# A hybrid decoder trunk on one core: VectorE work moved behind GpSimd's powers, attention ranked ahead, staged loads and first splits reordered

## The chip, the core and the metric

The kernel runs on one core of a Trainium2 chip. The core has a matrix engine (TensorE, in the profile PE, its weight loads PEld), a vector engine (VectorE, DVE), a scalar engine (ScalarE, ACT), a slower general engine (GpSimd, POOL) and an engine that only issues DMAs here (SyncE, SP). Each engine works through its own instructions in order, and waits on semaphores of the others. The metric is the device time of one execution in microseconds; the kernel before and the changed kernel are compared by their medians.

## The reference, cut to what matters

Two layers of a decoder trunk, 512 tokens of width 1024, all in float32:

```python
for l in range(2):
    h = rms_norm(x, ln_mix[l])
    proj = h @ w_in[l]                     # split into the inputs of four mixers and the gates g
    y_a = gelu(a_u) * (tril(sgu_w) @ rms_norm(gelu(a_v), sgu_norm) + sgu_b)   # gMLP, chunks of 128
    y_b = dsa_attention(q, k, v, qi, ki, wi)   # q, k normed and rotated; an indexer keeps 128 keys a query
    y_c = sigmoid(c_o) * rms_norm(mlstm_chunkwise(...), mlstm_norm)           # chunks of 128
    y_d = d_b * causal_conv3(d_c * d_x)
    x += (sum_n sigmoid(g_n) * (y_n @ w_branch[l, n])) @ w_out[l]
    h = rms_norm(x, ln_mlp[l])
    x += relu(h @ w_up[l]) ** 2 @ w_down[l]    # hidden width 4096
```

The norms use 1/sqrt(mean of squares + 1e-6). The indexer's score of a query against the keys before it is sum_h w_h relu(qi_h . ki), and the 128 best keys are kept for queries from position 128 on.

## The kernel before, in words

**Layout.** Activations lie feature-major: eight tiles of 128 features by 512 tokens. Every product of float32 operands is three matmuls: each operand is split into a high and a low part (hh and hl for h, whi and wlo for weights), and high·high, high·low and low·high are added up in PSUM (`mm3`).

**Weights.** A weight chunk (1024 or 1280 columns by 128 partitions) goes through `next_w`: SP loads it into `raw` (two buffers), ACT casts `whi<-raw`, DVE subtracts `wlo<-raw,whi` (three buffers each). The end of `wlo` frees the raw buffer, and so lets SP's next weight load start. These three steps are under high priority (`HP`).

**Order of the work.** The program is written once in Python; a scheduler then sets each engine's order from data dependencies and priorities. The stream of big products is the main line. Everything else (rotations, the indexer, top-k, mLSTM chunks, softmax) is written as generators in a list `side`; `tick()`, called after each half of a product's matmuls, lets each generator go one step, up to its next `yield`. While it does, the wrapper `Paced` ties every side instruction to the latest matmul of the main line (`at["mm"]`) by a dependency that only the scheduler sees, so that side work isn't ordered ahead of its place. `Ahead` is another wrapper, for DVE and ACT: it puts one tenth of the urgent priority around each call; the mLSTM uses it before the change. All instructions issued through such a wrapper carry the wrapper's line, L139, in the profile.

**One layer of the mixer.** Token-major projections come first (`tok_proj`, tile `tk`: 512, 336, 512 columns), then feature-major ones (`fm_proj`, tile `fm`), and again token-major ones. `qk_prep` norms and rotates q (i = 0) and k (i = 1): squares, `ssq` sums, a power on POOL (`rpow`), the products `rr` and `rt` of the rotation, times ssq, transposes on PE (`qkT`). For q, ssq is also multiplied by −0.125. The powers of all norms run on POOL.
The gMLP: its gate input v lies in two tiles v20 and v21, each with two chunks of tokens side by side. `vs` holds the chunks' mean squares; after the power on POOL, four scalings multiply v by vs and 0.5, written inline on the main line. `sgu_mix`, a side generator, then multiplies the triangular matrices `wt` by v on PE (`mix`, 16 small matmuls for each of two feature tiles i).
The indexer's top-k works on a score tile `sco` with DVE alone: 16 rounds for each block of 128 queries, of MAX (the eight largest into `m`) and MATCH_REPLACE (which strikes them out; a value load goes ahead of it).
mLSTM: per chunk a state, numerators `nd`, the result `hc`; its norm is `dn`, with a power on POOL and a scaling by 0.5, then hc·dn, then times (1 + tanh of the output gate) into `h2`; `finish` transposes h2 and multiplies it by `mlstm_norm`.
Then the gates (`gates`, tiles `g` and `p`, DVE's `gs` and `mg`), with attention (`lg`, softmax in `L`, transposes `pT`, `av`) between them, and the product with w_out (`wo`).

**The MLP** runs in three passes of 12, 12 and 8 tiles of the hidden width. In each, pairs of up tiles (`up`) come first; then the down projection (tiles `q` and `r` of PE) in a form with seven products in place of eight for each 2×2 of blocks. Its weights are staged: `load` brings blocks of w_down into six buffers `cr`, by SP, or by POOL's queue (always where a load adds onto a tile), and DVE adds some; `use` splits and multiplies one. `chain` is the tile that goes through block 11, 11+12, then plus 22, then plus 21; `b22` is block 22, and in the last pass, of 8 tiles, `sum2` is block 22 plus block 12, loaded over POOL's queue. In the two passes of 12 tiles nkp is 3, in the last 2. Results of a pass are kept in DRAM (`sum_dram`), the last pass folds them into x.

**The start.** The first product's weights go chunk by chunk with x: `first_loads(k0)`, called ahead of the split of chunk k0, loads the tiles of x that the chunk needs and norms them; the first two weight chunks are in `raw01`.

Of the kernel before, what the change touches and what calls it, by code (L numbers as in the profile page):

```python
# [21 lines left out]
P = 128  # L22
# [144 lines left out]
def trunk(tc, x_in, wall, consts, lps, sgus, out):  # L167
# [5 lines left out]
    with ExitStack() as es:  # L173
# [189 lines left out]
        def mlp(l, hh, hl, r2, gain):  # L363
# [10 lines left out]
            with tc.tile_pool(name="ap", bufs=1) as ap:  # L374
# [6 lines left out]
                for p, nt in enumerate(PASSES):  # L381
                    nk = nt // 2
                    ah, al = [], []
                    for t in range(nk):
                        F = ap.tile([P, 4, 256], F32, name="F", tag="F")
                        G_ = ap.tile([P, 4, 256], F32, name="Fs", tag="Fs")
                        ah.append(ftile("ah", f"ah{t}"))
                        al.append(ftile("al", f"al{t}"))
                        for i in range(2):
                            w_h, w_l = next_w()  # L390
                            pt = mmtile("up")
                            fm_group(pt, w_h, w_l, hh, hl)
                            a = flat(F[:, 2 * i:2 * i + 2])
                            with HP():
                                S.activation(a, pt, AF.Relu)
                                S.activation(a, a, AF.Square)
                        with HP():
                            S.copy(ah[t][:, 0:3], F[:, 1:4])
                            V.tensor_sub(G_[:, 0:2], F[:, A21:A21 + 1].to_broadcast([P, 2, 256]), F[:, A11:A22 + 1])
                            V.tensor_sub(G_[:, 2], F[:, A11], G_[:, 1])  # L400
                            V.tensor_sub(G_[:, 3], F[:, A12], G_[:, 2])
                            S.copy(ah[t][:, 3:7], G_)
                            V.tensor_sub(al[t][:, 0:3], F[:, 1:4], ah[t][:, 0:3].bitcast(F32))
                            V.tensor_sub(al[t][:, 3:7], G_, ah[t][:, 3:7].bitcast(F32))
# [24 lines left out]
                    def load(dst, i, j, k, add=False, eng=nc.sync):  # L429
                        with HP():  # L430
                            if add:
                                nc.gpsimd.dma_start(dst, piece(i, j, k), accum_op=ALU.add)
                            else:
                                eng.dma_start(dst, piece(i, j, k))
# [94 lines left out]
                    for k in range(nkp):  # L529
                        load(chain[k], 1, 1, k)  # L530
# [19 lines left out]
                    if 3 * nkp <= 6:  # L550

                        sum2 = [ap.tile([P, 1024], F32, name="cr", tag="cr", bufs=6) for _ in range(nkp)]
                        for k in range(nkp):
                            load(sum2[k], 2, 2, k, eng=nc.gpsimd)
# [100 lines left out]
def mixer(tc, em, env):  # L655
# [41 lines left out]
    def tok_proj(n, kk, chunks, tags, before=None, order=KORD[0]):  # L697
        pts = {c: mmtile("tk", tags[i]) for i, c in enumerate(chunks)}
        kks = kk if isinstance(kk, tuple) else (kk,) * (KD // kk)
        for k0, kk in zip(np.cumsum((0,) + kks), kks):  # L700
            w_h, w_l = next_w(before(k0) if before else None)
            assert not env["at"]["fold"] or order[k0] > 3
# [64 lines left out]
    else:  # L767
# [3 lines left out]

        def first_loads(k0):
            ks = {0: (0, 1), 1: ()}.get(k0, (k0, k0 + 1))
            for k in ks:
                x0.append(rtile("x0").bitcast(F32))
                with HP():
                    nc.sync.dma_start(x0[k], x_in[k])
                acc[:] = [norm(x0, lp("ln_mix"), hh, hl, (k,), *acc, sq_hp=False, sq_tile=et)]
            return raw01[:, k0] if k0 < 2 else None

        pq = tok_proj(512, G1K[0], [1, 2, 3], MM4, first_loads)
# [96 lines left out]
    def attention(sel, yb):  # L878
        Ls, pTs = {}, {}
# [101 lines left out]
    def mlstm(yc):  # L981
        V, S = Ahead(tc, env["V"]), Ahead(tc, env["S"])

        def finish(c, h2):
            pk = mmtile("hT", "ms")
            mn = lp("mlstm_norm")
# [7 lines left out]
        ip, gc, gi = lfs  # L994

# [48 lines left out]
        for c in range(4):  # L1044
# [61 lines left out]
            V.tensor_scalar(dn, dn, 0.5, None, ALU.mult)  # L1106
            V.tensor_mul(hc, hc, dn.unsqueeze(2).to_broadcast([P, 4, 64]))
            h2 = hc.rearrange("p h d -> p (h d)")
            V.scalar_tensor_tensor(h2, to[:, c], 1.0, h2, ALU.add, ALU.mult)
            yield from wait(3)  # L1110
# [28 lines left out]
    def qk_prep(i, n, src):  # L1139
# [9 lines left out]
        if i == 0:  # L1149
            V.tensor_scalar(ssq, ssq, -0.125, None, ALU.mult)  # L1150
# [103 lines left out]
    for c in range(4):  # L1254
        s_ = slice((c % 2) * 256, (c % 2) * 256 + 256)
        V.tensor_scalar(v2[c // 2][:, s_], v2[c // 2][:, s_], vs[:, c:c + 1], 0.5, ALU.mult, ALU.mult)
# [190 lines left out]
```

## Time and profile before

| | |
|---|---|
| runs of the kernel before | 1593.58 us median of three (1592.1 to 1593.97) |
| the profiled execution's own time | 1594.98 us |
| its span, first to last instruction | 1593.2 us |
| granted TensorE clock, mean | 0.999 |
| busy, share of the span | PE 99%, PEld 82%, DVE 70%, ACT 44%, POOL 8% |
| DMA | 198.91 MB, 125 GB/s in the mean |
| largest groups on PE | up, g, q, r, tk: 512-column matmuls, 0.39 us each as modelled, pipelined |
| largest groups on DVE | wlo<-raw,whi: 221, 282.9 us; wlo<-cr,whi: 96, 117.0 us |

A row of a timeline gives start, length (both us), engine, line, operation, output<-inputs, shape, how many in a row, and in brackets the idle time before it and what ended that. Matmuls overlap: the length of one is modelled, the distance of two starts is what it costs. The tile names in the rows are the program's, so a wait can be found in the code by its tile.

### The profile page before, as it was taken

The numbers are of one execution on the slowest core, as the hardware profiler recorded it, in microseconds if no ns is written. First come the engines' busy times: TensorE is split into PE (matmuls) and PEld (weight loads), VectorE is DVE, ScalarE is ACT, GpSimd is POOL, SyncE is SP. The second block draws the span as 40 slices with busy tenths as digits, with TensorE's granted clock in tenths as the row PEclk, the third lists the DMA queues.
The fourth block names the chain that finished last, engine by engine and source line by source line (L and its number), as shares of the span: only waits on it lengthen the run. The fifth ranks groups of instructions, "written<-read, shape, count | busy, mean of one in ns | idle before, by whom it ended". The sixth has DMA issues, their size and how long they took to land.

```text
span 1593.2 us, 20154 instructions
## 1 busy us (share of the span) xinstructions
PE 1580.3 (99%) x7584; PEld 1303.7 (82%) x7584; DVE 1109.5 (70%) x1893; ACT 708.2 (44%) x1056; POOL 122.2 (8%) x153
## 2 busy tenths in 40 slices
PE   9999999999999999999999999999999999999999
PEld 7788887878888888878888888887888888888887
DVE  6799997555555665655987999975555557556568
ACT  5454224423336545635554532354233455455362
POOL 1221000000000100020013120000000001001200
PEclk9999999999999999999999999999999999999999
DMA  7433322242353473387345233232423534724962
GB/s 192 128 100 104 103 92 91 84 135 100 100 187 129 71 233 99 74 210 213 93 130 137 85 110 106 83 99 76 143 96 107 199 105 71 233 94 79 239 184 80
DMA packets 67058, 198.91 MB, mean 125 GB/s; under 512 B 7616, under 2 KB 14848, under 8 KB 66960
## 3 DMA queue, kind: packets, MB, share of 16 engines
q1 hardware_dynamic: 54160, 167.15, 32.0%
q0 software_dynamic: 11936, 29.45, 10.2%
q8 instruction: 60, 0.98, 0.2%
q10 hardware_dynamic: 864, 1.01, 0.2%
q14 instruction: 38, 0.31, 0.1%
HBM read 177.10 MB, written 16.81 MB: 122 GB/s over the span
## 4 chain that ended last, share of the span: by engine, by line
PE 71%; DVE 17%; issue 6%; DMA 4%; POOL 2%; ACT 1%; ACTq 0%; DVEq 0%; POOLq 0%
PE up L139 22%; PE g L139 15%; PE q L139 10%; PE r L139 7%; PE wo L139 5%; PE p L139 4%; DVE wlo L139 4%; DVE sco L139 3%; PE tk L139 3%; DMA raw<-in_wall_dram 2%; DVE m L139 2%; PE fm L139 1%; DVE X L139 1%; ACT whi L139 1%; DVE rr L139 1%
## 5 line engine op out<-in xcount | busy, mean ns | idle before, releaser
L139 DVE TENSOR_TENSOR wlo<-raw,whi 128x1024 fp32r<-128x1024 f32 (+3 forms) x221 | 282.9, 1280 | 150.0 <-ACT whi L139 149.7
L139 ACT CAST whi<-raw 128x1024 fp32r<-128x1024 f32 (+3 forms) x220 | 241.1, 1096 | 252.1 <-DMA raw<-in_wall_dram 64.9
L139 PE MATMUL g<-hh,whi 128*128 128x512 f32 x512 | 200.6, 392 | 0.0
L139 PE MATMUL up<-hh,whi 128*128 128x512 f32 x512 | 199.5, 390 | 0.7 <-ACT whi L139 0.7
L139 PE MATMUL up<-hh,wlo 128*128 128x512 f32 x512 | 199.3, 389 | 0.5 <-DVE wlo L139 0.5
L139 PE MATMUL g<-hh,wlo 128*128 128x512 f32 x512 | 199.5, 390 | 0.0
L139 PE MATMUL g<-hl,whi 128*128 128x512 f32 x512 | 199.4, 389 | 0.0
L139 PE MATMUL up<-hl,whi 128*128 128x512 f32 x512 | 199.2, 389 | 0.0
L139 DVE TENSOR_TENSOR wlo<-cr,whi 128x1024 fp32r<-128x1024 f32 x96 | 117.0, 1221 | 75.9 <-ACT whi L139 75.8
L139 ACT CAST whi<-cr 128x1024 fp32r<-128x1024 f32 x96 | 100.9, 1053 | 120.7 <-PE r L139 45.0
L139 ACT ACTIVATE gs<-gs 128x512 f32<-128x512 f32 x64 | 40.6, 634 | 195.6 <-DVE gs L139 195.4
L139 PEld LDWEIGHTS up<-hh,whi 128*128 128x128 f32 x512 | 96.1, 188 | 21.1 <-ACT whi L139 1.2
L139 PEld LDWEIGHTS up<-hh,wlo 128*128 128x128 f32 x512 | 96.1, 188 | 20.9 <-DVE wlo L139 1.0
L139 PEld LDWEIGHTS g<-hh,wlo 128*128 128x128 f32 x512 | 96.1, 188 | 20.2
L139 PEld LDWEIGHTS g<-hh,whi 128*128 128x128 f32 x512 | 96.1, 188 | 20.2 <-issue 0.3
L139 PEld LDWEIGHTS up<-hl,whi 128*128 128x128 f32 x512 | 96.1, 188 | 19.9
L139 PEld LDWEIGHTS g<-hl,whi 128*128 128x128 f32 x512 | 96.2, 188 | 19.3
L139 PE MATMUL tk<-whi,hh 128*128 128x512 f32 (+2 forms) x304 | 108.3, 359 | 0.3 <-DVE whi L139 0.3
L139 PE MATMUL tk<-wlo,hh 128*128 128x512 f32 (+2 forms) x304 | 106.9, 355 | 0.0
L139 PE MATMUL tk<-whi,hl 128*128 128x512 f32 (+2 forms) x304 | 105.9, 352 | 0.0
L139 PE MATMUL q<-whi,ah 128*128 128x512 f32 (+1 forms) x260 | 100.4, 390 | 0.0
L139 PE MATMUL q<-wlo,ah 128*128 128x512 f32 (+1 forms) x260 | 100.4, 386 | 0.0
(287 smaller groups left out, 3040.7 us busy)
## 6 DMA issues: line engine op xcount, KB each, us to landing
raw<-in_wall_dram SPq DMA_DIRECT2D x147, 512.0 KB, 3.5
raw<-in_wall_dram SPq DMA_DIRECT2D x64, 640.0 KB, 3.8
cr<-in_wall_dram POOLq DMA_DIRECT2D x36, 512.0 KB, 5.4
cr<-in_wall_dram SPq DMA_DIRECT2D x32, 512.0 KB, 5.1
x<-in_x_dram SPq DMA_DIRECT2D x16, 256.0 KB, 5.0
xm_dram<-x SPq DMA_DIRECT2D x16, 256.0 KB, 2.0
sum_dram<-co SPq DMA_DIRECT2D x16, 256.0 KB, 4.4
sum_dram<-co POOLq DMA_DIRECT2D x16, 256.0 KB, 6.9
```

What stands on the lines that cost most here:

```text
L139: r = f(*a, **k)
```

## The change

It touches five places.

1. **v2_scale.** The four scalings of v leave the main line and become a side generator: two steps of waiting, then one scaling a step.
2. **qk_prep, q alone.** The multiplication of ssq by −0.125 goes from DVE to POOL, behind the power.
3. **mLSTM and attention.** The factor 0.5 leaves dn and goes into `mnh`, half of mlstm_norm, formed once a layer on POOL; the product of hc with the output gate is written between the power and the product with dn. Attention's DVE and ACT calls are wrapped in `Ahead`.
4. **Staged loads.** The loads of `chain` (block 11) and of `sum2` (block 22) get a scheduler-only dependency on `early`, the last main-line matmul before the last pair of up tiles.
5. **The start.** For the first chunk, the norm of x tile 0 and the load and norm of tile 1 are written behind the split of the weights.

```diff
--- before.py
+++ after.py
@@ -386,6 +386,7 @@
                         G_ = ap.tile([P, 4, 256], F32, name="Fs", tag="Fs")
                         ah.append(ftile("ah", f"ah{t}"))
                         al.append(ftile("al", f"al{t}"))
+                        early = at["mm"]
                         for i in range(2):
                             w_h, w_l = next_w()
                             pt = mmtile("up")
@@ -426,12 +427,15 @@
                         o = base + (((i - 1) * 2 + j - 1) * nkp + k) * sz
                         return wall[o:o + sz].rearrange("(p l) -> p l", l=1024)
 
-                    def load(dst, i, j, k, add=False, eng=nc.sync):
+                    def load(dst, i, j, k, add=False, eng=nc.sync, behind=None):
+
                         with HP():
                             if add:
-                                nc.gpsimd.dma_start(dst, piece(i, j, k), accum_op=ALU.add)
+                                r = nc.gpsimd.dma_start(dst, piece(i, j, k), accum_op=ALU.add)
                             else:
-                                eng.dma_start(dst, piece(i, j, k))
+                                r = eng.dma_start(dst, piece(i, j, k))
+                        if behind is not None:
+                            tc.add_manual_dep(ins_of(r), ins_of(behind).name, V._dep, reason="pace")
 
                     def form(f, bank, b, w_h, w_l, k, first, o=slice(0, T)):
                         for i in range(2):
@@ -527,7 +531,7 @@
                     U = [hpool.tile([P, T], F32, name="U", tag=n) for n in ("acc", "sq")]
                     chain = [ap.tile([P, 1024], F32, name="cr", tag="cr", bufs=6) for _ in range(nkp)]
                     for k in range(nkp):
-                        load(chain[k], 1, 1, k)
+                        load(chain[k], 1, 1, k, behind=early)
                         use(A11, A, chain[k], k, True)
                     with HP():
                         for b in range(2):
@@ -551,7 +555,7 @@
 
                         sum2 = [ap.tile([P, 1024], F32, name="cr", tag="cr", bufs=6) for _ in range(nkp)]
                         for k in range(nkp):
-                            load(sum2[k], 2, 2, k, eng=nc.gpsimd)
+                            load(sum2[k], 2, 2, k, eng=nc.gpsimd, behind=early)
                             load(sum2[k], 1, 2, k, True)
                     for k in range(nkp):
                         load(b22[k], 2, 2, k)
@@ -694,11 +698,13 @@
         for _ in range(n):
             yield
 
-    def tok_proj(n, kk, chunks, tags, before=None, order=KORD[0]):
+    def tok_proj(n, kk, chunks, tags, before=None, order=KORD[0], behind=None):
         pts = {c: mmtile("tk", tags[i]) for i, c in enumerate(chunks)}
         kks = kk if isinstance(kk, tuple) else (kk,) * (KD // kk)
         for k0, kk in zip(np.cumsum((0,) + kks), kks):
             w_h, w_l = next_w(before(k0) if before else None)
+            if behind:
+                behind(k0)
             assert not env["at"]["fold"] or order[k0] > 3
             if kk == 1:
 
@@ -769,16 +775,29 @@
         x0, acc = [], []
         raw01 = yp.tile([P, 2, T], F32R, name="raw01", tag="yh", bufs=3).bitcast(F32)
 
+        def load_x(k):
+            x0.append(rtile("x0").bitcast(F32))
+            with HP():
+                nc.sync.dma_start(x0[k], x_in[k])
+
+        def norm_x(k):
+            acc[:] = [norm(x0, lp("ln_mix"), hh, hl, (k,), *acc, sq_hp=False, sq_tile=et)]
+
         def first_loads(k0):
-            ks = {0: (0, 1), 1: ()}.get(k0, (k0, k0 + 1))
-            for k in ks:
-                x0.append(rtile("x0").bitcast(F32))
-                with HP():
-                    nc.sync.dma_start(x0[k], x_in[k])
-                acc[:] = [norm(x0, lp("ln_mix"), hh, hl, (k,), *acc, sq_hp=False, sq_tile=et)]
+
+            for k in {0: (0,), 1: ()}.get(k0, (k0, k0 + 1)):
+                load_x(k)
+                if k > 0:
+                    norm_x(k)
             return raw01[:, k0] if k0 < 2 else None
 
-        pq = tok_proj(512, G1K[0], [1, 2, 3], MM4, first_loads)
+        def first_norms(k0):
+            if k0 == 0:
+                norm_x(0)
+                load_x(1)
+                norm_x(1)
+
+        pq = tok_proj(512, G1K[0], [1, 2, 3], MM4, first_loads, behind=first_norms)
         load_consts()
         rs, rb = rstd(acc[0], 0)
     qr = {}
@@ -876,6 +895,7 @@
         V.tensor_scalar(sco, sco, SENT, BIG, ALU.not_equal, ALU.mult)
 
     def attention(sel, yb):
+        V, S = Ahead(tc, env["V"]), Ahead(tc, env["S"])
         Ls, pTs = {}, {}
 
         def softmax(j, b, r):
@@ -983,7 +1003,7 @@
 
         def finish(c, h2):
             pk = mmtile("hT", "ms")
-            mn = lp("mlstm_norm")
+            mn = mnh
             for j in range(2):
                 ptr(pk[:, blk(j)], h2[:, blk(j)])
             for j in range(2):
@@ -992,6 +1012,9 @@
                 V.scalar_tensor_tensor(yl, pk[:, blk(j)], mn[:, j:j + 1], yh.bitcast(F32), ALU.mult, ALU.subtract)
 
         ip, gc, gi = lfs
+
+        mnh = tt([P, 2], "mnh")
+        G.tensor_scalar(mnh, lp("mlstm_norm"), 0.5, None, ALU.mult)
 
 
         ms8 = tt([4, 8], "ms8")
@@ -1103,11 +1126,11 @@
             V.tensor_reduce(dn, nd[:, :, 0:64], AX.X, ALU.add)
             V.tensor_scalar(dn, dn, 1.0 / 64, EPS, ALU.mult, ALU.add)
             rpow(dn, dn)
-            V.tensor_scalar(dn, dn, 0.5, None, ALU.mult)
-            V.tensor_mul(hc, hc, dn.unsqueeze(2).to_broadcast([P, 4, 64]))
             h2 = hc.rearrange("p h d -> p (h d)")
             V.scalar_tensor_tensor(h2, to[:, c], 1.0, h2, ALU.add, ALU.mult)
-            yield from wait(3)
+            yield
+            V.tensor_mul(hc, hc, dn.unsqueeze(2).to_broadcast([P, 4, 64]))
+            yield from wait(2)
             if prev is not None:
                 finish(*prev)
             prev = (c, h2)
@@ -1147,7 +1170,7 @@
         V.tensor_scalar(ssq, ssq, 1.0 / 64, EPS, ALU.mult, ALU.add)
         rpow(ssq, ssq)
         if i == 0:
-            V.tensor_scalar(ssq, ssq, -0.125, None, ALU.mult)
+            G.tensor_scalar(ssq, ssq, -0.125, None, ALU.mult)
         rots = []
         for c2 in range(2):
             r_, t = et("rr"), et("rt")
@@ -1251,9 +1274,16 @@
             S.activation(t[:, s_], v2[c2][:, s_], AF.Square, accum_out=vs[:, c:c + 1])
     V.tensor_scalar(vs, vs, 1.0 / 1024, EPS, ALU.mult, ALU.add)
     rpow(vs, vs)
-    for c in range(4):
-        s_ = slice((c % 2) * 256, (c % 2) * 256 + 256)
-        V.tensor_scalar(v2[c // 2][:, s_], v2[c // 2][:, s_], vs[:, c:c + 1], 0.5, ALU.mult, ALU.mult)
+
+    def v2_scale():
+        yield
+        yield
+        for c in range(4):
+            s_ = slice((c % 2) * 256, (c % 2) * 256 + 256)
+            V.tensor_scalar(v2[c // 2][:, s_], v2[c // 2][:, s_], vs[:, c:c + 1], 0.5, ALU.mult, ALU.mult)
+            yield
+
+    side.append(v2_scale())
     wt = et("wt")
     bb = et("bb")
     nc.scalar.dma_start(wt, sgus[l, :, 0:512])
```

DVE, layer 0, where the powers of vs come back (`v` are the two tiles of the gMLP's gate input, `vs` their scale, `sco` and `m` the top-k's tiles). Before:

```order
L139 TENSOR_SCALAR vs<-vs 128x4
L139 TENSOR_TENSOR gu<-gu,u_1501 128x512
L139 TENSOR_SCALAR v_1412<-v_1412,vs 128x256 x2
L139 TENSOR_TENSOR u_1544<-fm,rb 128x512
L139 TENSOR_SCALAR v_1413<-v_1413,vs 128x256 x2
L139 TENSOR_TENSOR wlo<-raw,whi 128x1024
L139 MAX m_1241<-sco_890 128x8
L139 SCALAR_TENSOR_TENSOR X<-X,c_gc,cst 128x128 x2
L139 TENSOR_TENSOR X<-X,S 128x2x128 x2
L139 TENSOR_TENSOR kw<-ktok,E_1311 128x256
L139 SCALAR_TENSOR_TENSOR X<-X,c_gc,cst 128x128 x2
L139 MATCH_REPLACE sco_890<-m_1241,sco_890 128x384
```

After, up to the same operations:

```order
L139 TENSOR_SCALAR vs<-vs 128x4
L139 TENSOR_TENSOR gu<-gu,u_1499 128x512
L139 MAX m_1241<-sco_890 128x8
L139 TENSOR_SCALAR v_1414<-v_1414,vs 128x256
L139 TENSOR_TENSOR u_1544<-fm,rb 128x512
L139 MATCH_REPLACE sco_890<-m_1241,sco_890 128x384
L139 TENSOR_TENSOR wlo<-raw,whi 128x1024
L139 SCALAR_TENSOR_TENSOR X<-X,c_gc,cst 128x128 x3
L139 TENSOR_TENSOR X<-X,S 128x2x128 x2
```

and some rows on, with the last two scalings:

```order
L139 MAX m_1241<-sco_890 128x8
L139 TENSOR_TENSOR gu<-gu,u_1544 128x512
L139 TENSOR_TENSOR wlo<-raw,whi 128x1024
L139 MATCH_REPLACE sco_890<-m_1241,sco_890 128x384
L139 SCALAR_TENSOR_TENSOR u_1544<-gu,u_1544 128x512
L139 MAX m_1241<-sco_890 128x8
L139 TENSOR_SCALAR v_1415<-v_1415,vs 128x256
L139 MATCH_REPLACE sco_890<-m_1241,sco_890 128x384
L139 TENSOR_SCALAR v_1415<-v_1415,vs 128x256
```

The four scalings stood within three rows; now MAX, MATCH_REPLACE, two weight splits, the gMLP's u and the mLSTM's X and kw stand between the first and the fourth. PE's rows are the same before and after.

DVE, layer 0, where q is normed (`rr` and `rt` are the parts of the rotation, `ssq` the sums of squares). Before:

```order
L139 TENSOR_SCALAR ssq<-ssq 128x16
L139 TENSOR_TENSOR rt<-qe_430,tab 128x4x32 x2
L139 TENSOR_SCALAR ssq<-ssq 128x16
L139 TENSOR_TENSOR rr<-qe_430,tab 128x256
L139 TENSOR_TENSOR rr<-rr,rt 128x256
L139 TENSOR_TENSOR rt<-qe_430,tab 128x4x32 x2
L139 TENSOR_TENSOR rr<-qe_431,tab 128x256
L139 TENSOR_TENSOR wlo<-raw,whi 128x1024
L139 TENSOR_TENSOR rr<-rr,rt 128x256
L139 TENSOR_TENSOR rt<-qe_431,tab 128x4x32
L139 TENSOR_TENSOR rr<-rr,ssq 128x512
```

After:

```order
L139 TENSOR_SCALAR ssq<-ssq 128x16
L139 TENSOR_TENSOR rt<-qe_430,tab 128x4x32 x2
L139 TENSOR_TENSOR rr<-qe_430,tab 128x256
L139 TENSOR_TENSOR rr<-rr,rt 128x256
L139 TENSOR_TENSOR rt<-qe_430,tab 128x4x32 x2
L139 TENSOR_TENSOR rr<-qe_431,tab 128x256
L139 TENSOR_TENSOR rr<-rr,rt 128x256
L139 TENSOR_TENSOR wlo<-raw,whi 128x1024
L139 TENSOR_TENSOR rr<-rr,ssq 128x512
```

The second TENSOR_SCALAR on ssq is gone from DVE, and what stood behind it moves up.

SP, layer 0, around the up weights of the MLP's first pass (L253 is the weight load of `next_w`, L434 and L436 that of `load`, L453 and L457 store the sums). Before:

```order
L253 DMA raw<-in_wall_dram 128x1024
L434 DMA cr<-in_wall_dram 128x1024 x3
L253 DMA raw<-in_wall_dram 128x1024
L434 DMA cr<-in_wall_dram 128x1024 x2
L253 DMA raw<-in_wall_dram 128x1024
L434 DMA cr<-in_wall_dram 128x1024
L253 DMA raw<-in_wall_dram 128x1024 x5
L434 DMA raw<-in_wall_dram 128x1024 x2
L434 DMA cr<-in_wall_dram 128x1024 x2
L453 DMA sum_dram<-co 128x512 x2
```

After:

```order
L253 DMA raw<-in_wall_dram 128x1024 x8
L436 DMA raw<-in_wall_dram 128x1024 x2
L436 DMA cr<-in_wall_dram 128x1024 x6
L457 DMA sum_dram<-co 128x512 x2
L436 DMA raw<-in_wall_dram 128x1024
L457 DMA sum_dram<-co 128x512 x2
```

The six cr loads stood between the loads of the up weights; now eight up loads and two raw loads of the down projection stand ahead of all six.

## The prediction

> **What bounds the kernel now.** I read the busy table first, then what TensorE (PE) waits for, then the chain of waits around each such wait, then the rows of VectorE (DVE) there.
>
> ```profile
> PE 1580.3 (99%) x7584; PEld 1303.7 (82%) x7584; DVE 1109.5 (70%) x1893; ACT 708.2 (44%) x1056; POOL 122.2 (8%) x153
> ```
>
> What PE waits for (engine and tile that wait, engine and tile waited for):
>
> ```profile
> PE pT L139 <- DVE L L139: 2.0, 2, 1.2
> PE qkT L139 <- ACT rel L139: 0.9, 2, 0.7
> PE up L139 <- ACT whi L139: 0.7, 1, 0.7
> PE up L139 <- DVE wlo L139: 0.5, 1, 0.5
> ```
>
> PE is busy 99% of the span, so time can be won only where PE waits, and any new wait of PE is paid in full. The waits above (total us, times, longest) lie in places that the change touches. The view counts a wait from the modelled end of the matmul before; what it costs is a little more, from start to start:
>
> ```profile
> 252.13 0.39 PE L139 MATMUL g<-hl,whi 128*128 128x512 f32 x1
> 252.36 0.39 PE L139 MATMUL g<-hh,wlo 128*128 128x512 f32 x1
> 253.92 0.30 PE L139 MATMUL pT<-cst,L 128*128 128x128 f32 x1 [1.17 <-DVE L L139]
> ```
>
> Matmuls of 512 columns start 0.23 us apart; pT starts 1.56 after g, so this wait costs 1.33 where the view says 1.17. I add 0.16 to each wait: pT 2.0 + 0.32 = 2.3 in two layers, qkT 0.9 + 0.32 = 1.2, up 0.7 + 0.5 + 0.32 = 1.5. Together 5.0 us is what removing them is worth.
>
> **The start.** The instructions of the five engines stand in the same order there, with the same waits, before and after. Cost: nothing.
>
> **The q scale goes to GpSimd (POOL).** Chain of waits from 60 to 75 us (start, length, what):
>
> ```profile
> 63.21 2.94 POOL ssq L139
> ...
> 67.75 1.14 DVE wlo L139
> ...
> 68.91 3.46 DMA raw<-in_wall_dram
> ...
> 72.45 1.05 ACT whi L139
> 73.50 0.29 ACT rel L139
> ...
> 73.83 0.66 PE qkT L139 x4
> ```
>
> DVE's rows there, and a row of PE and of DVE from later on:
>
> ```profile
> 66.18 0.17 DVE L139 TENSOR_SCALAR ssq<-ssq 128x16 f32<-128x16 f32 x1 [2.60 <-POOL ssq L139]
> ...
> 69.34 0.68 DVE L139 TENSOR_TENSOR rr<-rr,ssq 128x512 f32<-128x512 f32 x1
> ...
> 83.75 0.39 PE L139 MATMUL fm<-hh,wlo 128*128 128x512 f32 x1
> 84.21 0.69 DVE L139 SCALAR_TENSOR_TENSOR ckT<-fm,rb 128x512 f32<-128x512 f32 x1
> ```
>
> DVE stands idle 2.60 us for POOL's power, and behind it in DVE's queue stands the split wlo, whose end lets the next weight load begin, after which come whi, rel and at last PE's qkT. With the scale on POOL, DVE goes on: wlo, the load and whi all come 2.5 us earlier, and qkT's wait (0.7 here, 0.2 in layer 1) is gone: −1.2. The next reader of ssq on DVE waits for POOL's second operation, ready at 66.15 plus less than one power (2.94), at the latest 69.1; DVE reaches that reader at 69.34 before and some 2 us earlier now, so DVE can lose up to 2 us again there. But wlo is ahead of it, so the gain of qkT stands.
> Does DVE's lead of 2.6 us carry on? At 84.21 ckT starts 0.07 us after the end of PE's last fm (83.75 + 0.39): there DVE waits for PE, and any lead ends. I take none from there on.
>
> **v is scaled behind the top-k work.** This decides the sum. DVE and PE in layer 0, then layer 1:
>
> ```profile
> 148.53 0.86 DVE L139 TENSOR_SCALAR v<-v,vs 128x256 f32<-128x256 f32 x2 [0.94 <-POOL vs L139]
> ...
> 149.90 0.60 DVE L139 TENSOR_SCALAR v<-v,vs 128x256 f32<-128x256 f32 x2
> ...
> 154.07 0.07 DVE L139 MATCH_VALUE_LOAD sco<-m,sco 128x8 f32 x1
> 154.14 0.53 DVE L139 MATCH_REPLACE8 sco<-m,sco 128x384 f32<-128x384 f32 x1
> 154.60 0.67 DVE L139 SCALAR_TENSOR_TENSOR u<-gu,u 128x512 f32<-128x512 f32 x1
> ...
> 159.32 0.07 DVE L139 MATCH_VALUE_LOAD sco<-m,sco 128x8 f32 x1
> 154.43 1.09 PE L139 MATMUL mix<-wt,v 128*64 128x128 f32 x16
> 155.46 0.50 PE L139 MATMUL fm<-hh,whi 128*128 128x512 f32 x1
> 940.18 0.85 DVE L139 TENSOR_SCALAR v<-v,vs 128x256 f32<-128x256 f32 x2 [0.94 <-POOL vs L139]
> 950.96 0.08 DVE L139 MATCH_VALUE_LOAD sco<-m,sco 128x8 f32 x1
> 947.44 0.50 PE L139 MATMUL fm<-hh,whi 128*128 128x512 f32 x1
> ```
>
> Before, the four scalings end at 150.50 (149.90 + 0.60) and PE's mix, which reads all four, starts at 154.43 without a wait. PE's order is the same after the change, so mix still stands ahead of fm and of all that follows. On DVE the first scaling starts where it did, since POOL's vs releases it; a MAX now fills that wait of 0.94 and costs nothing. But from the first to the fourth scaling DVE now issues exactly what it issued before from 148.53 up to 159.32, and two more MATCH_REPLACE with their value loads (0.53 each, 154.07 to 154.60). DVE has no other gap there. So the fourth scaling ends at 159.32 + 1.06 + 0.08 (an operation ends 0.08 after the next one starts: 0.86 for two, next at 0.78) = 160.46. PE then has the last four of the sixteen mix matmuls left (1.03 / 4 = 0.26, of 154.43 to 155.46) and a signal of about 0.05: fm starts at 160.77 in place of 155.46. **+5.3 us.** Layer 1, in the same way: 950.96 + 1.06 + 0.08 + 0.26 + 0.05 = 952.41 against 947.44: **+5.0**.
> Behind mix on PE stands everything else, so nothing hides this. What it gives: DVE gets 5 us nearer to PE. At 252 PE waited 1.33 us for DVE's L; now DVE is there first, and both pT waits go: −2.3. The bound on the other side: if DVE, too, is held up by PE's pause, they stay, +2.3.
>
> **mLSTM and attention.** One scaling per chunk leaves DVE, and hc times the gate is placed in POOL's power:
>
> ```profile
> 247.11 0.18 DVE dn L139
> ```
>
> Eight chunks at 0.18 take 1.4 us off DVE. PE waits for DVE in that stretch only at pT, which is already counted; attention's own order on DVE and ScalarE (ACT) is nearly the old one. Worth 0, at most a share of those 2.3.
>
> **Staged loads of the down projection.** On SP, and on POOL's queue in the third pass, the cr loads now come behind all loads of the up weights. The chain of waits at the third pass of layer 0 has this piece:
>
> ```profile
> 702.19 9.43 DMA raw<-in_wall_dram
> ```
>
> The page's table of DMA issues (count, size, middle time to landing), SP's queue, the tile cr and PE's first q in the first pass:
>
> ```profile
> raw<-in_wall_dram SPq DMA_DIRECT2D x147, 512.0 KB, 3.5
> cr<-in_wall_dram SPq DMA_DIRECT2D x32, 512.0 KB, 5.1
> 512.72 6.09 SPq L434 DMA_DIRECT2D raw<-in_wall_dram  x2
> L139 ACT CAST whi<-cr x5: 1039/1055/1056, 521.3 to 537.9; 128x1024 fp32r<-128x1024 f32 x5
> L432 POOL DMA_DIRECT2D cr<-in_wall_dram x3: 850/865/957, 524.2 to 534.7; - x3
> 532.16 0.39 PE L139 MATMUL q<-whi,ah 128*128 128x512 f32 x1
> ```
>
> The load that PE waits for at 711 takes 9.43 us where 3.5 is the middle value: cr loads run beside it. They now come after it, so it lands about 6 us earlier, and the two up waits go: −1.5 (layer 0 alone; none in layer 1).
> The price: in the first pass six cr loads now start at 512.72 + 6.09 = 518.8. The first lands 5.1 later, at 523.9; ACT's first cast of it moves from 521.3 to about 524, q needs it (cast 1.05, split 1.2) by 532.16: 6 us to spare. POOL's first accumulating load moves 3 us as well, from 524.2 to 527.2; it lands 5.3 to 7.1 later (the view of that tile), at the latest at 534.3, and its cast stood at 537.9 at the latest: 1.4 to 3.6 us to spare. So I cost it at 0. If that cover is not there, each of six passes waits 1 to 1.4 us: 6 to 8.
>
> **The clock.** While PE waits for the third scaling it stands still for long. The second is done near 154.6, the third near 159.6 (one scaling and one MATCH_REPLACE before the end), so it idles 4.6 us in one piece, longer than anything since the start.
>
> ```profile
> 2.72 2.74 PE L139 MATMUL warm<-warm 128*128 128x512 bf16 x6 [2.72 <-ACT warm L139]
> 1588.50:1591.50 3.00, 0.91 (x6) 0.47 (x5) 1.32 (x3) 0.00 (x0) 0.00 (x0) 1.00 0.65 203
> 1591.50:1593.20 1.70, 0.00 (x0) 0.00 (x0) 0.00 (x0) 0.00 (x0) 0.00 (x0) 0.51 0.20 58
> ```
>
> At the start, matmuls begin 0.43 to 0.47 us apart (six in 2.74) rather than 0.23, for some 4.5 us. At the end, PE works 0.91 of 3 us, and then the granted clock is half (0.51). A pause of 4.6 us can thus close the clock, and PE would run at half speed for a while: 0 to 2.2 us (half of 4.5) lost each time. I take 1.0 in each layer: +2.0.
> [...]
>
> **Sum**, against the profiled execution's own 1594.98 us (span 1593.2): + 5.3 + 5.0 − 1.2 − 2.3 − 1.5 + 2.0 = +7.3, 1602.3. The median of the runs, 1593.58, is 1.4 below that execution; from it, 1600.9. I predict **1601**.
>
> **The rivals**, from the median.
> 1. *The clock stays open.* Same waits without the 2.0: 1598.9. For it: nothing of the kind follows the pause of 1.33 us at pT; against it: the end rows. [...] 20%.
> 2. *The lead carries on.* DVE keeps its 2.6 us in each layer, less the 1.2 that PE gains: 4.0 off the 10.3. [...] For it: DVE is the engine that is late here. Against it: ckT at 84.21 waits for PE. 9%.
> 3. *The other side: faster.* DVE gets through so early that mix finds its four scalings. Place: the fourth, needed at 155.2 (155.46 less 0.26) and by my count done at 160.46. Done before 157.7 (2 × 2.5 = 5.0) the stalls cost less than is saved, before 156.1 (2 × 0.9 = 1.8) by more than 3.2; at 155.2 only the savings are left: 1588.6. For it: the scalings are released by POOL, and DVE's top-k steps have no reader soon. Against it: a queue without gaps, in order. 5%.
> 4. *The staged loads come late*, 6 more beside the forecast: 1606.9. For it: six loads at once on one queue, and 5.1 may grow to the 9.43 above. Against it: 6 us to spare at q. 6%.
> The forecast itself: 60%.
>
> **Range and chances.** The forecast alone holds 1599 to 1604 (clock term from 0 to 2.2 each, pT kept or not). With the rivals: 1596 to 1605, which leaves out the third, most of the fourth and half of the second. A change of 0.2%, 3.2 us, is about what a measurement of this kernel can tell from none: faster is below 1590.4, slower above 1596.8. The forecast, 1 and 4 are slower: 0.86; 2 is the same: 0.09; 3 is faster: 0.05.
>
> **What would show it.** Right: PE waits of about 5 us at mix, on DVE's v, once a layer, with fm behind it; no waits at pT, qkT and up; a granted clock under 1 just after each mix; wlo before 66 us. Wrong: v's fourth scaling before 157 us, mix's wait small, a PE wait at q or r on cr, or pT's wait still there.

## The result and the profile after

The changed kernel takes 1615.95 us (median of four runs, 1613.76 to 1616.97) against 1593.26 us of the kernel before on the same chip: a ratio of 1.0141, 95% interval 1.0124 to 1.0159. It is slower, as forecast, but by 22.7 us where 7.4 were forecast, and far outside the range of 1596 to 1605.

The profiled execution has a span of 1615.1 us, 21.9 more than before. What PE waits for now (engine and tile that wait, engine and tile waited for: total us, times, longest):

```profile
PE q L139 <- ACT F L139: 9.6, 2, 5.7
PE mix L139 <- DVE v L139: 9.2, 3, 4.5
PE fm L139 <- ACT vt L139: 0.4, 1, 0.4
```

The waits at pT, qkT and up of before are gone, all three. Two new ones stand in their place, of nearly the same size: mix, which the prediction had, and q in the last pass of the down projection, which it had costed at nothing.

**The first loss, mix.** DVE's scalings and PE's rows around mix, layer 0 and then layer 1:

```profile
147.26 0.35 DVE L139 TENSOR_SCALAR v<-v,vs 128x256 f32<-128x256 f32 x1 [0.47 <-POOL vs L139]
...
152.91 0.34 DVE L139 TENSOR_SCALAR v<-v,vs 128x256 f32<-128x256 f32 x1
...
157.82 0.34 DVE L139 TENSOR_SCALAR v<-v,vs 128x256 f32<-128x256 f32 x1
...
158.60 0.35 DVE L139 TENSOR_SCALAR v<-v,vs 128x256 f32<-128x256 f32 x1
152.59 0.44 PE L139 MATMUL mix<-wt,v 128*64 128x128 f32 x4
...
158.22 1.48 PE L139 MATMUL mix<-wt,v 128*64 128x128 f32 x8 [4.47 <-DVE v L139]
159.63 0.80 PE L139 MATMUL fm<-hh,whi 128*128 128x512 f32 x1
...
164.16 0.69 PE L139 MATMUL intra<-vaug,X 128*64 128x65 f32 x16
954.15 0.68 PE L139 MATMUL mix<-wt,v 128*64 128x128 f32 x8
...
965.72 0.69 PE L139 MATMUL intra<-vaug,X 128*64 128x65 f32 x16
```

From the first scaling's start to the fourth's end DVE takes 11.7 us (147.26 to 158.95); the count from the rows of before had said 11.9. In layer 0 PE needs 7.0 us from mix to fm (152.59 to 159.63) in place of 1.03. The last eight matmuls of mix alone take 1.48, and fm too is slow. The granted clock (last column but two; here in layer 1) says why:

```profile
954.00:958.00 4.00, 0.83 (x9) 0.40 (x8) 4.00 (x11) 2.18 (x3) 0.00 (x0) 1.00 0.00 0
958.00:962.00 4.00, 2.60 (x11) 1.68 (x12) 3.93 (x11) 0.00 (x0) 0.00 (x0) 0.54 0.41 131
962.00:966.00 4.00, 4.00 (x18) 2.86 (x19) 3.13 (x6) 0.62 (x1) 0.00 (x0) 0.60 0.47 159
```

Before and after, PE runs the same 7584 matmuls in the same order, so a loss can be counted from the starts of the same matmuls in both profiles. Twelve fm matmuls follow on mix, and then `intra`, of the mLSTM. Before, it stands here in layer 0:

```profile
158.40 0.69 PE L139 MATMUL intra<-vaug,X 128*64 128x65 f32 x16
```

From mix to intra PE took 3.97 us before (154.43 to 158.40, in layer 1 946.41 to 950.38) and takes 11.57 now, in both layers (152.59 to 164.16, 954.15 to 965.72). So mix costs 7.6 us in each layer. With the clock kept open (a_warm, below) it costs 5.3 and 5.7, so the half clock is 2.3 and 1.9 of it.

**The second loss, q.** The chain of waits before the down projection of layer 0's last pass (start, length, what), and PE's rows where it ends:

```profile
719.08 9.48 DMA raw<-in_wall_dram
...
731.00 11.59 DMA raw<-in_wall_dram
...
749.54 1.23 DVE wlo L139
...
750.78 0.33 SPq L436
...
751.20 4.39 DMA cr<-in_wall_dram
...
758.23 5.41 DMA cr<-in_wall_dram
...
763.72 1.04 ACT whi L139
...
765.31 9.79 PE q L139 x31
```

SP issues chain's loads only at 751.20, right behind a raw load at 750.78 that had waited for a raw buffer (the wlo that ends at 750.77 frees it). The first lands at 755.60. Then chain has to be split, POOL adds block 12 to it (758.23, 5.41 us), and the sum is cast at 763.72. PE had run out of q matmuls at 760.94.

```profile
760.94 0.39 PE L139 MATMUL q<-whi,ah 128*128 128x512 f32 x1
765.31 0.80 PE L139 MATMUL q<-whi,ah 128*128 128x512 f32 x1 [3.98 <-ACT F L139]
```

The wait is 4.1 us (765.31 − 760.94 − 0.23), in layer 1 5.8; with the half clock behind it, 6.6 and 7.8 by the starts of the same matmuls. (The view names ACT's F as the releaser. In ACT's queue F stands directly behind the cast of the sum, and it is the cast that had waited, for the DMA.)

Together, by the starts of the same matmuls: 7.6 + 7.6 + 6.6 + 7.8 = 29.6 lost; won 1.4 at qkT, 2.4 at pT, 1.9 at up and 1.3 at fm, 7.0 in all, and 0.7 in small amounts elsewhere. The difference is the 21.9 of the spans.

### The profile page after: what moved, and what is told of

It reads as the page before. It is cut to its first block, busy times and chain, and to the rows that moved or that the text cites. A ratio compares the mean times of both kernels' runs of the same rounds, so it can differ in the third digit from the quotient of the medians.

```text
span 1615.1 us, 20162 instructions
## 1 busy us (share of the span) xinstructions
PE 1588.5 (98%) x7584; PEld 1309.4 (81%) x7584; DVE 1112.0 (69%) x1883; ACT 711.4 (44%) x1056; POOL 122.6 (8%) x157
## 4 chain that ended last, share of the span: by engine, by line
PE 84%; DMA 6%; DVE 6%; ACT 1%; issue 1%; POOL 1%; SPq 0%; ACTq 0%; POOLq 0%; DVEq 0%
PE g L139 22%; PE up L139 16%; PE q L139 11%; PE r L139 8%; PE fm L139 7%; PE p L139 5%; PE wo L139 5%; PE tk L139 5%; DMA raw<-in_wall_dram 4%; DVE wlo L139 2%; DMA cr<-in_wall_dram 1%; DVE sco L139 1%; ACT whi L139 1%; PE ix L139 1%; PE lg L139 1%
## 5 line engine op out<-in xcount | busy, mean ns | idle before, releaser
L139 DVE TENSOR_TENSOR gs<-g,rb 128x512 f32<-128x512 f32 x64 | 44.2, 690 | 87.6 <-PE g L139 87.3
```

What stands on the lines that cost most here:

```text
L139: r = f(*a, **k)
```

## The experiments

Theory: two separate losses, mix (late scalings) and q (late staged loads), each with a half clock behind it. Rivals: one loss that only shows in several places, or lateness that moves elsewhere. Every ratio is to the kernel before, run beside it on the same chip; 0.001 is 1.6 us. The runs were made on several chips, on which the kernel before took 1595.0 to 1597.5 us, so from run to run the ratios compare and the times do not.

| run | what it is | ratio | 95% interval |
|---|---|---|---|
| a_vinline | changed, v scaled inline | 1.0052 | 1.0037 to 1.0067 |
| a_nostage | changed, staged loads free | 1.0057 | 1.0041 to 1.0072 |
| a_neither | changed, without either | 0.9978 | 0.9969 to 0.9987 |
| b_ssq | before, q scale on GpSimd | 0.9987 | 0.9979 to 0.9996 |
| b_att | before, mLSTM and attention | 0.9997 | 0.9988 to 1.0006 |
| a_chainfree | a_vinline, chain's loads free | 0.9984 | 0.9975 to 0.9993 |
| a_warm | changed, PE kept busy in the pause | 1.0111 | 1.0097 to 1.0125 |
| c_one1 | one step for v; chain before the second up pair of the last pass | 0.9998 | 0.9989 to 1.0007 |
| c_t0 | the same, chain before the first pair | 0.9988 | 0.9979 to 0.9996 |
| c_free | one step for v, staged loads free | 0.9974 | 0.9964 to 0.9984 |

### One loss at a time

a_vinline takes the generator back:

```diff
-    def v2_scale():
-        yield
-        yield
-        for c in range(4):
-            ...
-            yield
-    side.append(v2_scale())
+    for c in range(4):
+        s_ = slice((c % 2) * 256, (c % 2) * 256 + 256)
+        V.tensor_scalar(v2[c // 2][:, s_], v2[c // 2][:, s_], vs[:, c:c + 1], 0.5, ALU.mult, ALU.mult)
```

> The changed kernel, with the four scalings of v written inline again as before. Theory (two separate losses: PE's mix waits for v's scalings, 14.9 us in the trace with the half clock behind them, and a wait of PE's q in the last pass of the down projection, 13.7 us): the waits at mix go, the two at q stay, 1615.95 - 14.9 = about 1601. Rival (VectorE is late by the same work wherever the scalings stand, and the lateness only moves): waits of 1.0 to 1.3 us come back at pT in both layers, about 1603.5. A second rival (the waits at q follow from the pauses at mix, as later shifts of the same engines): the q waits go too, about 1588.

Measured: 1604.26 us, 1.0052. The mix waits are gone, the q waits stay. PE's waits:

```profile
PE q L139 <- ACT F L139: 7.8, 2, 4.3
PE pT L139 <- DVE L L139: 0.7, 2, 0.4
```

So q does not follow from the pauses at mix. A part of the rival is true: pT waits a little again (0.7 in the view where 2.0 stood before), because PE no longer pauses and DVE is late again.

a_nostage takes the dependency off both loads:

```diff
-                        load(chain[k], 1, 1, k, behind=early)
+                        load(chain[k], 1, 1, k)
...
-                            load(sum2[k], 2, 2, k, eng=nc.gpsimd, behind=early)
+                            load(sum2[k], 2, 2, k, eng=nc.gpsimd)
```

> The changed kernel, without the scheduling dependency on the staged loads (chain and sum2 free as before). Theory: the two q waits of the last pass (4.1 and 5.8 us, with the half clock behind them 13.7) go, the wait at the first up weights of layer 0's last pass (1.5 us) comes back, the mix waits stay: 1615.95 - 13.7 + 1.5 = about 1603.8. Rival (the q waits come from something else, such as the order of the sums' accumulating stores): they stay, about 1616.

Measured: 1604.38 us, 1.0057. q is gone, mix stays, and the wait at up is back:

```profile
PE mix L139 <- DVE v L139: 8.1, 2, 4.4
PE up L139 <- ACT whi L139: 1.6, 1, 1.6
PE up L139 <- DVE wlo L139: 0.5, 1, 0.5
```

In this profile the clock closed behind the waits at up as well (last section).

a_neither has both diffs.

> The changed kernel without either: v scaled inline, staged loads free. What is left are the q scale on GpSimd, the mLSTM and attention edits and the start. Theory (the losses add): 1615.95 - 14.9 - 13.7 + 1.5 = about 1588.9, faster than the 1593.26 of before, with waits left at up of layer 0's last pass, and perhaps at pT. Rival (what is left is worth nothing but the qkT wait): 1592.0.

Measured: 1591.52 us, 0.9978, 3.5 us faster than before. The losses add: 1.0052 + 1.0057 − 0.9978 = 1.0131, next to the 1.0141 of the whole change. Each of the two edits costs 0.0074 to 0.0079 (12 to 13 us) on top of the rest. The gain is a little less than expected (4.4 us, 1588.9 from 1593.26); pT and up still wait.

### What the rest is worth

b_ssq is the kernel before with one word changed:

```diff
         if i == 0:
-            V.tensor_scalar(ssq, ssq, -0.125, None, ALU.mult)
+            G.tensor_scalar(ssq, ssq, -0.125, None, ALU.mult)
```

> The kernel before, with the q scale on GpSimd alone. Theory: qkT's wait goes (1.2 us in two layers), and the shorter wait at fm (1.35 us in two layers in the trace after) is this edit's too, since it sits 4 us ahead of the same power: 1593.26 - 2.5 = about 1590.7. Rival (the fm gain belongs to another edit): 1592.0, with fm's waits as before (1.3 and 0.5 us in the view of waits).

Measured: 1593.68 us, 0.9987, 2.1 us faster, between the theory's 2.5 and the rival's 1.3. qkT waits no more; pT and fm (1.1 in all) wait less than before (2.0 and 1.8), and up waits more (0.7 before):

```profile
PE pT L139 <- DVE L L139: 1.2, 2, 0.7
PE up L139 <- ACT whi L139: 1.1, 1, 1.1
```

fm does not settle it. In the profiles of this study its total lies between 0.4 and 3.5 us, so single profiles can't give its gain to an edit.

b_att is the kernel before with the edits of mLSTM and attention:

```diff
     def attention(sel, yb):
+        V, S = Ahead(tc, env["V"]), Ahead(tc, env["S"])
...
-            V.tensor_scalar(dn, dn, 0.5, None, ALU.mult)
-            V.tensor_mul(hc, hc, dn.unsqueeze(2).to_broadcast([P, 4, 64]))
             ...
             V.scalar_tensor_tensor(h2, to[:, c], 1.0, h2, ALU.add, ALU.mult)
-            yield from wait(3)
+            yield
+            V.tensor_mul(hc, hc, dn.unsqueeze(2).to_broadcast([P, 4, 64]))
+            yield from wait(2)
```

> The kernel before, with the mLSTM and attention edits alone (factor 0.5 moved, product with the output gate behind the power, attention under the raised priority). Theory (worth nothing, as predicted): 1.000 of before, with the waits at pT of 2.0 us in the view still there. Rival (they take VectorE's lateness at pT away): the pT waits shrink by 1 to 2 us, 0.9990.

Measured: 1596.28 us, 0.9997 (0.9988 to 1.0006): no difference that can be told. In its one profile the pT waits are down to 0.8 us in total, as the rival had it. The interval holds the theory's 1.000 and the rival's 0.9990, so the time decides between them no more than one profile does.

### Which staged load, and why

a_chainfree is a_vinline with chain's loads free and only sum2's tied.

```diff
-                        load(chain[k], 1, 1, k, behind=early)
+                        load(chain[k], 1, 1, k)
```

> The changed kernel with v scaled inline and the loads of chain free again; only sum2's loads keep the dependency. Theory (order: q waits because chain's loads stand in SyncE's queue behind two raw loads, of which the second waits for a buffer): the q waits of 3.7 to 4.5 us that remained with v inline are gone, and the time is that without either edit or a little less, 0.9970 to 0.9980 of before. Rival (contention: sum2's loads over GpSimd's queue beside the last up weights make those land after 9 to 12 us and push everything behind them): PE still waits at up or at q of the last pass, 1.003 or more.

Measured: 1594.78 us, 0.9984. The waits of 3.7 to 4.5 us are gone. Small ones are left at q and r, 2.1 us in layer 0 and 1.3 in layer 1 by the starts of the same matmuls, and none at up:

```profile
PE q L139 <- DVE al L139: 1.1, 2, 0.6
```

So chain's place in SP's queue makes the large wait. It shows in ACT's casts, here of a_vinline, where the first cast of chain waits for its load, and the second, of the sum, for POOL's:

```profile
751.15 1.05 ACT L139 CAST whi<-cr 128x1024 fp32r<-128x1024 f32 x1 [3.22 <-DMA cr<-in_wall_dram]
...
759.23 1.04 ACT L139 CAST whi<-cr 128x1024 fp32r<-128x1024 f32 x1 [3.97 <-DMA cr<-in_wall_dram]
```

And of the kernel before, where both wait for PE instead, so the tiles are early:

```profile
746.39 1.05 ACT L139 CAST whi<-cr 128x1024 fp32r<-128x1024 f32 x1 [1.32 <-PE up L139]
...
757.27 1.05 ACT L139 CAST whi<-cr 128x1024 fp32r<-128x1024 f32 x1 [3.09 <-PE up L139]
```

c_one1 and c_t0 move chain's loads of the last pass forward in two steps, leave the other loads free, and do all four scalings of v in one step of the generator after one step of waiting. The diff is that of c_one1; c_t0 has t == 0:

```diff
     def v2_scale():
-        yield
         yield
         for c in range(4):
             ...
-            yield
+        yield
...
-                        early = at["mm"]
+                        if t == 1:
+                            early = at["mm"]
...
-                        load(chain[k], 1, 1, k, behind=early)
+                        load(chain[k], 1, 1, k, behind=early if p == last else None)
...
-                            load(sum2[k], 2, 2, k, eng=nc.gpsimd, behind=early)
+                            load(sum2[k], 2, 2, k, eng=nc.gpsimd)
```

> The changed kernel with the side generator for v kept, but one step of waiting in place of two and all four scalings in that one step; the dependency of the staged loads only in the last pass, for chain alone, and on the last matmul before its second pair of up tiles. Theory (what counts is where the fourth scaling stands in VectorE's queue, and that chain's loads are ahead of the last raw loads): by the rows the fourth scaling is done at 154.1, before the 155.2 at which mix needs it; no wait at mix, none at q, none at up of layer 0's last pass: 1.5 us below the version without either edit, 0.9968 of before. Rival (chain's loads, now beside the loads of sums and of x in the last pass, come late or make the raw loads late): waits of 1 to 2 us at up or q, 0.9980 or more.

> As the version with all four scalings in one step, but chain's loads of the last pass tied to the last matmul before its first pair of up tiles in place of the second. Theory (the q waits grow with the place of chain's loads in SyncE's queue: 4 us behind the last up weights, 1.5 to 2.1 us among the last ones, 0.0 where they are free): here they stand among the fourth to seventh up loads, so the q and r waits come to under 1 us a layer, the up wait of 1.5 us stays away, and the time is 0.9970 to 0.9980 of before. Rival (any loads of staged tiles beside the loads of sums and x cost as much as they save): 0.9990 or more.

Measured: 1595.76 us, 0.9998, and 1592.81 us, 0.9988. In both mix waits no more and up neither; q still does. c_one1, then c_t0, which also waits 0.8 us for DVE's al:

```profile
PE q L139 <- ACT F L139: 2.9, 4, 1.0
```

```profile
PE q L139 <- ACT F L139: 3.7, 4, 1.5
```

Both theories were misses: c_one1 had expected no wait at q, and c_t0 under 1 us a layer at q and r. c_one1 lies in its rival's range, c_t0 between its theory's (up to 0.9980) and its rival's (from 0.9990), nearer the rival's. By the starts of the same matmuls, staged loads that share the last pass with the loads of sums and of x cost 2.6 to 3.9 us a layer at q and r, and save 1.8 at up in layer 0. In c_t0 chain is in time, but the last up weights, issued at 729.55, land after 13.4 us, and ACT, which casts them before it can cast cr, comes late to the first q. In the kernel before, with the loads free, the last up load (issued at 737.02) lands after 3.4 us. So there are two ways to lose here: chain's place in the queue (the large one) and traffic on the DMA engines (2.6 to 3.9 us a layer, with the small waits behind q and at r).

c_free has the same generator and free loads everywhere.

> As the version with all four scalings in one step, with the staged loads free everywhere, as before. Theory (one step is early enough for mix, so this side generator costs nothing): no wait at mix, none at q, the up wait of 1.6 us in layer 0 as before; the time is that of the version with v inline and free loads, 0.9975 to 0.9985 of before. Rival (GpSimd's wait filled with top-k work brings VectorE ahead, so the pT waits go as well): 0.9965 to 0.9975.

Measured: 1590.56 us, 0.9974 (0.9964 to 0.9984): 4.2 us faster than the kernel before, and the lowest ratio here. It lies at the border of theory (from 0.9975) and rival (to 0.9975), and the interval covers both; its profile shows the rival's mechanism, no wait at pT at all. DVE's scalings and PE's mix in layer 0:

```profile
146.63 0.35 DVE L139 TENSOR_SCALAR v<-v,vs 128x256 f32<-128x256 f32 x1 [0.47 <-POOL vs L139]
...
151.21 0.87 DVE L139 TENSOR_SCALAR v<-v,vs 128x256 f32<-128x256 f32 x3
152.39 1.09 PE L139 MATMUL mix<-wt,v 128*64 128x128 f32 x16
153.41 0.50 PE L139 MATMUL fm<-hh,whi 128*128 128x512 f32 x1
```

The fourth scaling is done at 152.08, 0.3 us before mix begins. So the generator in one step costs nothing. Whether it wins anything beside the version with v inline (0.9978) can't be told from these intervals; the second step of waiting and a step for each scaling are what made it a loss.

### The clock

a_warm is the changed kernel with matmuls in the pause, whose results nothing reads:

```diff
                 pmm(pt[half(j), blk(c)], v2[c // 2][:, o:o + 64], wtv[:, g])
+            if i == 0 and c == 1:
+                pd = mmtile("dummy", "ms", env["turn"]["ms"])
+                for _ in range(18):
+                    pmm(pd, hh[0][:, 0:P], hh[0])
```

> The changed kernel, with 18 matmuls of 512 columns on PE between the second and the third chunk of the first mix, into a tile that nothing reads: 18 x 0.227 = 4.1 us, inside the pause of 4.7 us. Theory (the clock closes in the pause): the pause stays as long, but mix's last matmuls and the fm matmuls behind it are at full pace, and about 1.9 us a layer are won, 3.8 in all: 1615.95 - 3.8 = about 1612. Rival (those matmuls are slow for another reason, such as weights that come late): nothing is won, 1616 or, as the added matmuls run past the scalings, some tenths more.

Measured: 1614.89 us, 1.0111: 0.0030 or 4.8 us less than the changed kernel, where 3.8 were expected. The two intervals (1.0097 to 1.0125 and 1.0124 to 1.0159) just touch, so the size is rough, and the trace carries the verdict: by the starts of the same matmuls the two mixes cost 5.3 and 5.7 us, 11.0 in place of 15.2. PE around the mix of layer 0, and the clock there:

```profile
155.35 0.73 PE L139 MATMUL mix<-wt,v 128*64 128x128 f32 x8
156.00 4.38 PE L139 MATMUL dummy<-hh 128*128 128x512 f32 x18
160.54 0.44 PE L139 MATMUL mix<-wt,v 128*64 128x128 f32 x4 [0.16 <-DVE v L139]
161.34 0.44 PE L139 MATMUL mix<-wt,v 128*64 128x128 f32 x4 [0.35 <-DVE v L139]
161.71 0.50 PE L139 MATMUL fm<-hh,whi 128*128 128x512 f32 x1
```

```profile
156.00:160.00 4.00, 4.00 (x20) 3.30 (x18) 4.00 (x9) 1.57 (x2) 0.00 (x0) 1.00 0.05 14
160.00:164.00 4.00, 3.49 (x20) 2.32 (x19) 3.93 (x10) 0.00 (x0) 0.00 (x0) 1.00 0.33 117
```

The pause is the same (fm starts 161.71 − 155.35 − 1.03 = 5.3 us late), but the clock stays at 1.00, and mix and fm run at full pace. So the slow matmuls behind the pause of the changed kernel are the clock, and not late weights.

## Why the prediction was wrong, point by point

- **The start: nothing.** No run speaks against it; it was not tried alone, since the instructions there are the same. After the first 10 us PE's matmuls start within 0.04 us of where they did, up to fm at 62 us.
- **The q scale: −1.2.** Right. The wait of 2.60 us on DVE is gone in the changed kernel, wlo starts before the power is back, and the next reader of ssq waits 0.16 us for POOL's second operation:

```profile
64.36 1.21 DVE L139 TENSOR_TENSOR wlo<-raw,whi 128x1024 fp32r<-128x1024 f32 x1
65.73 0.69 DVE L139 TENSOR_TENSOR rr<-rr,ssq 128x512 f32<-128x512 f32 x1 [0.16 <-POOL ssq L139]
```

  Alone it gave 2.1 us. That DVE's lead ends at ckT held: DVE waits there for PE, and at mix it was as late as counted:

```profile
82.34 0.69 DVE L139 SCALAR_TENSOR_TENSOR ckT<-fm,rb 128x512 f32<-128x512 f32 x1 [0.57 <-PE fm L139]
```

- **v behind the top-k work: +5.3 and +5.0.** Right in place, cause and size. With the clock kept open (a_warm) the pauses are 5.3 and 5.7 us, and taking the generator back is worth 0.0089 in all (1.0141 to 1.0052), 14 us with the clock and against pT's return.
- **pT: −2.3.** Right in the changed kernel: no wait is left. The reason holds only in part. With the pauses taken away (a_vinline) 0.7 of the 2.0 us comes back, and in c_free, which has no pause at mix, nothing does; so other edits share in it (b_ssq leaves 1.2, b_att 0.8), and that the whole gain came as forecast is partly luck.
- **mLSTM and attention: 0.** Right within what can be measured (0.9997).
- **up of the last pass: −1.5.** Right: the wait goes with the dependency (1.9 us by the starts of the same matmuls) and comes back without it.
- **The clock: 1.0 in each layer.** Right that it closes, under-sized: 2.3 and 1.9, about the upper bound of 2.2. And it closed at q as well, four times in all.
- **Staged loads: "So I cost it at 0".** This is the step that failed, and it alone puts the time outside the range: the two q waits cost 14.4 us with their half clock, and without the dependency (a_nostage) 1.0057 of 1593.26 is 1602.3, inside it. The spare time (6 us at q, 1.4 to 3.6 at the sum) was worked out from the rows of the first pass, and then taken for all six. The last pass is another case. Its weights share the DMA engines with loads of the sums and of x, and sum2's loads were pushed into the same stretch: two up loads there took 9.5 and 11.6 us, which took 8.7 and 5.9 before, and from 735 to 740 us the DMA share is 1.07, where it was 0.57. And chain stands behind two raw loads, of which the second waits for a buffer, so it starts at 751.20, not with the last up weights. In the first pass the same two raw loads were read from a row (512.72, 6.09) and counted; the last pass's counterpart did not enter the count.
- **The rivals.** The fourth had the place right (staged loads late), gave it 6 us and 6%. It was spread over six passes at 1 us each; in fact two passes pay 4.1 and 5.8, and the others nothing. Its row against, 6 us to spare at q, was the first pass's again. The first, second and third are out. The second, 10.3 − 4.0 = 6.3 us of pauses over two layers, is "the same" only without the clock's 2.0; no run shows that such pauses leave the clock open, and in a_warm a wait of 2.2 us closed it (last section).

With the clock at 2 and the loads at 14.4, the forecast's sum reads 10.3 − 5.0 + 4.0 + 14.4 = 23.7; the fm waits, shorter by 1.3 in that one profile, bring it to 22.4, and the medians differ by 22.7.

What is open: how the 14.4 divide between queue order and traffic. a_chainfree shows that chain's place makes the large wait; in c_one1 and c_t0, with chain further ahead, 2.6 to 3.9 us a layer remain, for which c_t0's rows show traffic. The two aren't independent, since the traffic also delays the raw loads that chain stands behind (in the changed kernel the up load of 731.00 lands after 11.6 us, its cast comes at 742.67, and the first of the two raw loads is issued at 745.01, before at 739.61).

## What to carry to other kernels

Where a load or a scaling is moved later, its spare time has to be read in every pass and stage in which it occurs, above all in the one with other traffic in the same queue: a mean, or the first instance, says nothing of the last. A queue makes a wait out of whatever stands ahead in it (here chain's loads were issued at 751.20, behind a raw load that had waited for its buffer until 750.78), so look for the instruction ahead that itself waits for a buffer. And filling one engine's wait with other work pays only while the work behind the wait keeps its place: here the same four scalings cost nothing in one step of the generator and 13 us over several.

## What the runs showed of the hardware that was not expected

The clock closes after shorter pauses than the 4.6 us of the forecast. All four pauses of the changed kernel (4.0 to 5.7 us in the view of waits) closed it, down to 0.50, and in a_vinline and a_nostage two pauses each (3.5 to 4.4 us) too, to 0.50 in a_vinline and, over the lowest 4 us of each, 0.55 and 0.50 in a_nostage. In a_warm's profile a wait of 2.2 us at fm did, far ahead of the added matmuls (PE's wait, and the clock behind it, last column but two):

```profile
PE fm L139 <- ACT vt L139: 3.5, 2, 2.2
```

```profile
64.00:65.00 1.00, 1.00 (x3) 0.81 (x4) 1.00 (x5) 0.00 (x0) 1.00 (x1) 0.52 0.00 0
```

Two short waits close together did, too: those at up, of 1.6 and 0.5 us in a_nostage and of 1.1 and 0.5 us in b_ssq, the latter 1.6 us of waiting between 708.92 and 711.25. The clock some 2 us behind them, a_nostage, then b_ssq:

```profile
721.00:722.00 1.00, 1.00 (x4) 0.79 (x3) 0.63 (x1) 0.93 (x2) 0.68 (x1) 0.50 1.01 393
```

```profile
713.00:714.00 1.00, 1.00 (x3) 0.74 (x3) 0.00 (x0) 0.98 (x2) 0.88 (x2) 0.50 0.96 356
```

There eight matmuls start 0.43 us apart, not 0.23, which costs some 1.6 us on top of the waits. In the kernel before, the same two waits, 0.7 and 0.5 us, left the clock open (1.00 from 710 to 720 us), and so did single waits of up to 1.5 us (q in c_t0, whose mean granted clock is 1.0). In the changed kernel half clock lasts 4.2 to 5.9 us from PE's first matmul behind the pause (158.22 to 163.05, 765.31 to 770.60, 959.30 to 965.15 and 1568.54 to 1572.75); in a_warm's profile it is some 3.5 us (0.52 from 64 to 65 us, 0.50 up to 67, 0.77 from 67 to 68). The end rows of the kernel before had pointed that way: PE's last matmul ends at 1589.99 there, and the clock is at half from 1591.55.
